# Near scores on full rows one head at a time, fewer opening dummies and a newly computed order in a one-core attention and convolution layer

## The chip, the cores and the metric

The kernel runs on 1 core of one Trainium2 chip. The metric is the device time of one execution in microseconds (us), as the median over the runs. Beside it stands one profiled execution with its trace; shares and durations come from that one.

## What is computed

One decoder layer over 1024 tokens of width 1024: a pre-norm, one combined input projection to 5632 columns, two branches, one output projection, the residual and a final norm. The attention branch mixes three dilated causal windows (128 with step 1, 512 with step 4, 2048 with step 16) by their softmax denominators; 16 query heads share 4 key heads. The convolution branch is a gated depthwise convolution of 31 taps, a layer norm and a gate.

```python
h = rmsnorm(x, norm_g)
proj = einsum('bsd,de->bse', h, w_in)            # 1024 x 1024 x 5632
q, k, v, a_gate, c_val, c_glu, c_gate = split(proj)
for window, dilation in ((128, 1), (512, 4), (2048, 16)):
    s = q k^T + alibi, causal and within the window, every dilation-th key
    m = max(s); p = exp(s - m); l = sum(p); o = p v / l; lse = m + log(l)
y_att = sum(softmax(lse) * o) * silu(a_gate)
c = conv1d(c_val * sigmoid(c_glu), conv_w) + conv_b
y_conv = silu(layernorm(c)) * silu(c_gate)
out = rmsnorm(x + concat(y_att, y_conv) @ w_out, final_norm_g)
```

## The kernel before

All float32 products are made of rounded parts. A value is split into a high part (fp32r) and a low part, the rest. A projection tile (`inproj`, tile names `ps`, `wh`, `wl`, `hhi`, `hlo`) adds three products of 512 columns into one PSUM bank, so that one block of 128 output columns takes 48 matmuls.

Attention works by pairs of heads (`attend(p)`, p from 0 to 7). The near scores of a query block of 128 tokens are taken against 256 keys, the far scores against every fourth key. The stationary operand of a score is `qs` (near) or `qf` (far): for head j of the pair, the 64 rows `r` from j x 64 hold the high part of the query, the other 64 rows its low part. `kdh` holds the high part of the keys on both halves of the rows, `kdl` their low part on both halves. In `score`, `first` is one matmul over all 128 rows for each unit (high and low query with the high key), and `second` adds the high query with the low key over 64 rows alone: rows 0 to 63 for head 0, rows 64 to 127 for head 1, so that `zip(*second)` issues the two heads' 64-row matmuls side by side. Each head has a PSUM bank of its own (`sc`, two in all). A near step has two query blocks of both heads: four full-row matmuls and then four of 64 rows, and it occurs four times for each pair, 32 times in all. The first of the four steps contains block 0, which has 128 keys in place of 256. On VectorE `add_min` then adds the bias and takes the least, and ScalarE takes the exponential.

Near and far results are exchanged through DRAM, the weights are transposed on TensorE (`tp_m`, `tp_s`, `tp_w`, `tp_p`), multiplied with the values (`on`, `of`) and gathered in `comb`.

The order of the whole program is written out by a planner, `Plan.order`. Every operation has an engine, a cost in us and a priority, its number less a boost (`pl.boost`, from `TUNE`). The planner takes the operation that can start first by its own model, and the program then holds each engine to that order. An engine's queue is in order, so whatever waits at its head holds up all behind it. The model counts for a DMA 1.1 us to its start, its bytes by a rate, and 0.9 us until its result counts as there (L395 to L397). `LIMITS` says how many buffers of a kind may be in use; most of them come from 33 slots of 4 KB a partition (`c4`). `SECTIONS` says which projection blocks (h and k, q, v, a, c by number) run beside which pair's attention: entry k runs beside `attend(k - 1)`, for k from 1 to 8; the convolution of `hc` k runs beside entries 0 to 7.

At the opening TensorE runs `WARM` transposes of the identity into a bank that nobody reads (tile `idle`), while the first rows of `x` come in. Behind them in its queue is the product that spreads `norm_g` over the partitions (`gbc`), for which the first scaling of `x` on VectorE waits. `MORE` adds dummies behind the transposes (`xT`) of the first two token blocks. `parameters` loads the convolution's rows (`rows`) with five small loads and transposes them (`par_ps`).

Near the end come `load_wo_att` (raw loads `raw_oa`, split into `woah` and `woal`), `layer_norm` by halves (`cc`, `mean`, `ss`, `var`, `rb`), the attention's output projection `att_part` (tile `opsa`, operand `ya` loaded from `y_dram`), and the convolution's (`opsc`). The load of `ya` names the last `woal` as something it comes after: `pl.load(y, ..., after=w[1][1][7] if last else z)`.

Of the kernel before, what the change touches and what calls it, by code (L numbers as in the profile page):

```python
# [31 lines left out]

LIMITS = {"x": 5, "raw": 1, "raw_oc": 1, "raw_oa": 2, "wh": 3, "wl": 3, "tab": 2, "e": 7, "pt": 4, "vs": 4, "vc":
          4, "turn": 2, "opsa": 2, "score": 2, "hc": 5, "c": 7, "t": 1, "g": 1, "gl": 7, "y": 2, "ag": 4, "cc": 5,
          "qs": 5, "qf": 4, "kdh": 9, "kdl": 6, "yc": 2, "ya": 2, "zc": 7, "za": 3}

RESERVE = {"e": 7, "pt": 3}
BANKS = {"mm": 3, "sc": 2, "tp": 2, "o": 1}  # L40
WARM = 55
LATE = C_CG + 6 * P
MORE = (10, 12)
TUNE = {"w": 195, "use": 240, "ln": 65, "att": 240, "conv": 5, "wo": 215, "woa": -20, "ap": 0, "wait": 0.2116}
SECTIONS = [("k0 q0 h1 v", 0), ("h2 a0 q1", 1), ("h3 a1 q2 a2", 1), ("q3 h4", 1), ("h5 k1 a3 q4", 1), ("h6 a4 q5",
            1), ("c0 h7 a5 q6", 1), ("c1 q7 a6 a7 c2 c3", 1), ("c4 c5", 1), ("c6 c7", 0)]


def score_tables():
# [112 lines left out]
class Plan:  # L162
    LATENCY = 0.2
    ahead = 267
    near = 574
# [138 lines left out]
    def order(self):  # L304
# [12 lines left out]
        held, inuse, taken, bank = set(), {}, {}, {}  # L317
# [7 lines left out]
        dma, table = 0.0, None  # L325
        out = []
        reserving = [i for i, op in enumerate(ops) if any(b.group in RESERVE for b in op[4])]
        first, last = reserving[0], reserving[-1]
# [31 lines left out]
        while len(out) < n:  # L360
            best = None
            for e, todo in ready.items():
                now, pick = None, None
                for i in sorted(todo, key=self.prio.__getitem__):
                    t = start_of(i)
# [12 lines left out]
            t, i = best  # L378
            e, cost, _, _, bufs = ops[i]
# [14 lines left out]
            done = end + self.LATENCY  # L394
            if e in ("SP", "POOL"):  # L395
                dma = max(dma, t + 1.1) + self.dma_time[i]
                done = dma + 0.9  # L397
            elif e == "DVE":
                done = end + 0.13
            for b in bufs:  # L400
# [63 lines left out]
def layer_kernel(tc, x, norm_g, w_in, conv_w, conv_b, ln_g, ln_b, w_out, fin_g, tab, out):  # L464
# [3 lines left out]
    def pool(name, space=None):  # L468
# [4 lines left out]
    pl = Plan(tc, {  # L473
        "big": (sb, "big", 4), "c8": (sb, "c8", 1), "c4": (sb, "c4", 33), "c2": (sb, "c2", 5), "st": (sb, "st", 16),
        "sx": (sb, "sx", 6),
        **{k: (ps, k, BANKS[k]) for k in PSUM_KINDS},
    }, LIMITS)

# [38 lines left out]
    def bank(kind, name, group=None):  # L517
        return pl.buf(kind, [P, 512], F32, name, group=group)
# [35 lines left out]
    raw, ready = {}, {}  # L554
# [106 lines left out]
    vs = [c4([P, 2, NKV, P], f"vs{i}", F32R) for i in range(4)]  # L661
    vc = [c4([P, 2, NKV, P], f"vc{i}", F32R) for i in range(4)]
# [39 lines left out]
    qs, qf = {}, {}  # L702
# [20 lines left out]
    ag = {}  # L723
# [15 lines left out]
    hc = {}  # L739
# [56 lines left out]
    def attend(p):  # L796
# [4 lines left out]
        kh, kl = kd[kv]  # L801
        y = c4([P, 4, 256], f"y{p}")
# [30 lines left out]
        def score(name, units):  # L833


            first, second, todo = [], [[], []], []
            for j in range(2):
                sc, o = bank("sc", f"sc{p}_{name}_{j}", "score"), 0
                for q, keys, t, e, s, near in units[j]:
                    dst = sc[:, o:o + e.cols]  # L840
                    to, r = dst.crossed() if near else dst, slice(j * DH, j * DH + DH)
                    first.append((to, q, keys(kh), not o, False))
                    second[j].append((to, q[r], keys(kl)[r], False, len(second[j]) == len(units[j]) - 1))
                    todo.append((e, dst, t, s))
                    o += e.cols
            pl.mm(first + [c for both in zip(*second) for c in both])
            for e, dst, t, s in todo:
                pl.add_min(e, dst, t, 3e38, s[:, 0])
                pl.act(e, e, AF.Exp, bias=s[:, 0], scale=-1.0, accum=s[:, 1])
# [13 lines left out]
        w = pl.buf("sx", [P, 4, 2, 2, 4], F32, f"w{p}")  # L863
        f = pl.buf("sx", [P, 4, 2, 4], F32, f"f{p}")
# [8 lines left out]
        both = f[:, :, 1, :]  # L873
# [291 lines left out]
```

## Time and profile before

| | us |
|---|---|
| median of 3 runs | 899.86 |
| lowest and highest | 898.11, 900.07 |
| profiled execution, device time | 898.14 |
| its span in the trace | 896.3 |
| TensorE busy in the span | 873.2 |
| VectorE busy | 655.8 |
| ScalarE busy | 592.8 |

The span is the time from the first to the last record of the core; 1.84 us of the profiled execution lie around it. A busy TensorE is not one at its peak, since matmuls are pipelined and their records overlap: the distance from one matmul's start to the next one's is what it costs the engine.

### The profile page before, as it was taken

The page shows a single profiled execution, that of the slowest core. Times are in us where ns is not written, and L with a number is a line of the kernel's source. Part 1 is how long each engine was busy: PE and PEld are TensorE (multiplying, and loading weights), DVE is VectorE, ACT ScalarE, POOL GpSimd, SP SyncE. Part 2 cuts the span into 40 slices and gives each one's busy share as a digit, 9 for nine tenths or more (in the row PEclk, how much of TensorE's full clock was granted, in tenths as well). Part 3 has the DMA queues.
Part 4 walks back from the last instruction along what each step waited for, and adds up shares of the span by engine and source line. Part 5 has one row for each costly group of instructions (what it writes and reads, how often), then busy time and mean ns, then how long its engine had stood idle before and what let it go on. Part 6 is the DMA issues. An engine that isn't in the chain of part 4 may idle for free.

```text
span 896.3 us, 13046 instructions
## 1 busy us (share of the span) xinstructions
PE 873.2 (97%) x4493; PEld 720.2 (80%) x4493; DVE 655.8 (73%) x1506; ACT 592.8 (66%) x1392; POOL 53.3 (6%) x69
## 2 busy tenths in 40 slices
PE   8999999999999999999999999999999799999996
PEld 7888888888888788887887887888787678878885
DVE  5769996689699689789989779943649895625333
ACT  4777368677958867977977947983896744414111
POOL 0001001010010010010010110101000000000000
PEclk9999999999999999999999999999999799999999
DMA  7533607254553474545355744455773697777111
GB/s 266 164 71 58 153 3 165 50 116 77 138 111 81 100 150 108 139 71 143 78 112 143 165 94 130 89 137 112 217 261 141 204 363 238 252 217 229 71 48 47
DMA packets 104953, 123.53 MB, mean 138 GB/s; under 512 B 17941, under 2 KB 78357, under 8 KB 104888
## 3 DMA queue, kind: packets, MB, share of 16 engines
q1 hardware_dynamic: 97000, 94.40, 34.3%
q0 software_dynamic: 7888, 28.32, 17.9%
q8 instruction: 35, 0.57, 0.3%
q14 instruction: 30, 0.25, 0.1%
HBM read 65.35 MB, written 24.84 MB: 101 GB/s over the span
## 4 chain that ended last, share of the span: by engine, by line
PE 86%; DMA 7%; DVE 3%; ACT 2%; issue 1%; SPq 1%; POOL 0%; DVEq 0%; ACTq 0%; POOLq 0%
PE ps L237 52%; PE opsc L237 10%; PE opsa L237 7%; PE sc_near L237 3%; PE on L237 3%; PE of L237 3%; PE sc_far L237 2%; DMA y<-comb 2%; PE tp_p L235 1%; PE tp_m L235 1%; DMA rows<-in_ln_b 1%; PE tp_s L235 1%; DMA raw_oc<-in_w_out 1%; ACT e L252 1%; DMA yc<-yc_dram 1%; DMA x<-in_x 1%
## 5 line engine op out<-in xcount | busy, mean ns | idle before, releaser
L237 PE MATMUL ps<-hhi,wh 128*128 128x512 f32 (+1 forms) x720 | 288.1, 401 | 0.3 <-ACT hhi L250 0.2
L237 PE MATMUL ps<-hlo,wh 128*128 128x512 f32 (+1 forms) x720 | 279.6, 390 | 0.3 <-DVE hlo L265 0.3
L237 PE MATMUL ps<-hhi,wl 128*128 128x512 f32 (+1 forms) x720 | 188.7, 395 | 0.0
L237 PEld LDWEIGHTS ps<-hhi,wh 128*128 128x128 f32 x720 | 135.6, 188 | 31.4 <-issue 0.5
L237 PEld LDWEIGHTS ps<-hlo,wh 128*128 128x128 f32 x720 | 135.8, 189 | 27.6 <-DVE hlo L265 0.8
L237 PEld LDWEIGHTS ps<-hhi,wl 128*128 128x128 f32 x720 | 129.3, 188 | 27.9
L252 ACT ACTIVATE e<-e,near 128x256 f32<-128x256 f32 (+1 forms) x256 | 115.6, 488 | 22.2 <-DVE near L265 12.3
L269 DVE SCALAR_TENSOR_TENSOR c<-hc,taps,c 128x511 f32<-128x511 f32 (+14 forms) x120 | 88.4, 737 | 0.3
L269 DVE SCALAR_TENSOR_TENSOR c<-t,taps,c 128x511 f32<-128x511 f32 (+14 forms) x120 | 88.6, 738 | 0.0
L269 DVE SCALAR_TENSOR_TENSOR t<-hc,taps,t 128x511 f32<-128x511 f32 (+6 forms) x112 | 82.5, 736 | 0.8 <-ACT t L252 0.8
L237 PE MATMUL opsc<-woc,yhc 128*128 128x512 f32 (+1 forms) x272 | 80.8, 381 | 0.0
L252 ACT ACTIVATE e<-e,far 128x224 f32<-128x224 f32 (+1 forms) x128 | 54.0, 424 | 36.0 <-DVE far L284 35.7
L298 POOL DMA_DIRECT2D wl<-raw x40 | 34.7, 868 | 452.1 <-ACT wl L252 350.1
L237 PEld LDWEIGHTS opsc<-woc,yhc 128*128 128x128 f32 x272 | 50.2, 188 | 10.6
L252 ACT ACTIVATE fjunk<-zc 128x512 bf16<-128x512 f32 (+1 forms) x17 | 10.3, 606 | 68.0 <-DVE zc L265 67.8
L237 PE MATMUL opsc<-woc,ylc 128*128 128x512 f32 (+1 forms) x136 | 52.0, 382 | 1.5 <-DVE ylc L265 1.5
L284 DVE CUSTOM_DVE_ANT_0 e<-sc_near,tab 128x256 f32<-128x256 f32 (+1 forms) x128 | 45.0, 404 | 9.9 <-PE sc_near L237 9.2
L250 ACT CAST wh<-raw 128x1024 fp32r<-128x1024 f32 x44 | 46.0, 1044 | 1.6 <-DMA raw<-in_w_in 1.4
L237 PE MATMUL opsa<-woah,yla 128*128 128x512 f32 x112 | 45.5, 406 | 1.5 <-DVE yla L265 1.5
L237 PE MATMUL opsa<-woah,yha 128*128 128x512 f32 x112 | 45.4, 405 | 0.0
L237 PE MATMUL opsa<-woal,yha 128*128 128x512 f32 x112 | 45.0, 402 | 0.0
L252 ACT ACTIVATE e<-e,f 128x96 f32<-128x96 f32 (+1 forms) x128 | 44.5, 439 | 0.2 <-DMA f<-back 0.2
(166 smaller groups left out, 1405.1 us busy)
## 6 DMA issues: line engine op xcount, KB each, us to landing
raw<-in_w_in SPq DMA_DIRECT2D x44, 512.0 KB, 4.5
wl<-raw POOLq DMA_DIRECT2D x40, 512.0 KB, 4.9
x<-in_x SPq DMA_DIRECT2D x8, 512.0 KB, 8.5
tab<-in_tab SPq DMA_DIRECT2D x8, 512.0 KB, 3.4
c_dram<-c SPq DMA_DIRECT2D x8, 512.0 KB, 3.3
g_dram<-g SPq DMA_DIRECT2D x8, 512.0 KB, 2.8
raw_oa<-in_w_out SPq DMA_DIRECT2D x8, 512.0 KB, 5.7
raw_oc<-in_w_out SPq DMA_DIRECT2D x8, 512.0 KB, 7.4
```

What stands on the lines that cost most here:

```text
L235: nc.tensor.transpose(out.ap(), a.ap(), b.ap())
L237: nc.tensor.matmul(out.ap(), a.ap(), b.ap(), start=start, stop=stop)
L250: nc.scalar.copy(out.ap(), x.ap())
L252: nc.scalar.activation(out.ap(), x.ap(), func, **{k: ap_of(v) for k, v in kw.items()})
L269: lambda: self.nc.vector.scalar_tensor_tensor(out.ap(), a.ap(), ap_of(s), b.ap(), op0, op1),
L284: lambda: self.nc.vector.tensor_tensor_reduce(out.ap(), a.ap(), b.ap(), 1.0, ap_of(first), ALU.add, ALU.min, least.ap()),
L298: self.op("POOL", 1.0, lambda: self.nc.gpsimd.dma_start(ap_of(dst), x.ap(), accum_op=ALU.add), [dst], [x, dst])
```

## The change

In `score`, a near unit is no longer put into `first` and `second`. For each head a list `one` takes, unit by unit, the full-row matmul with `kdh` and right behind it a full-row matmul with `kdl`, and each head's list is an operation of its own. (The low query times the low key comes along with it.) Far units stay as they were, over 64 rows side by side. `WARM` goes from 55 to 26 and `MORE` from (10, 12) to (8, 8). The planner counts 1.9 in place of 0.9 us at the end of a DMA. Limits, priorities and sections are other numbers: the loads and splits of `load_wo_att` have a boost of -350 in place of -20, `att_part` one of 50 in place of 0; the blocks a2 and c3 move by one section to later ones, `yc` has one buffer in place of two, `tab` one in place of two.

```diff
 LIMITS:
-  "wh": 3, "tab": 2, "hc": 5, "qs": 5, "kdl": 6, "yc": 2, "zc": 7
+  "wh": 4, "tab": 1, "hc": 7, "qs": 6, "kdl": 5, "yc": 1, "zc": 8
-WARM = 55
+WARM = 26
-MORE = (10, 12)
-TUNE = {"w": 195, "use": 240, "ln": 65, "att": 240, "conv": 5, "wo": 215, "woa": -20, "ap": 0, "wait": 0.2116}
-SECTIONS = [("k0 q0 h1 v", 0), ("h2 a0 q1", 1), ("h3 a1 q2 a2", 1), ("q3 h4", 1), ("h5 k1 a3 q4", 1), ("h6 a4 q5",
-            1), ("c0 h7 a5 q6", 1), ("c1 q7 a6 a7 c2 c3", 1), ("c4 c5", 1), ("c6 c7", 0)]
+MORE = (8, 8)
+TUNE = {"w": 225, "use": 120, "ln": 75, "att": 240, "conv": 15, "wo": 165, "woa": -350, "ap": 50, "wait": 0.2116}
+SECTIONS = [("k0 q0 h1 v", 0), ("h2 a0 q1", 1), ("h3 a1 q2", 1), ("a2 q3 h4", 1), ("h5 k1 a3 q4", 1), ("h6 a4 q5",
+            1), ("c0 h7 a5 q6", 1), ("a6 c1 a7 q7 c2", 1), ("c5 c4 c3", 1), ("c6 c7", 0)]
...
                 dma = max(dma, t + 1.1) + self.dma_time[i]
-                done = dma + 0.9
+                done = dma + 1.9
...
             for j in range(2):
-                sc, o = bank("sc", f"sc{p}_{name}_{j}", "score"), 0
+                sc, o, one = bank("sc", f"sc{p}_{name}_{j}", "score"), 0, []
                 for q, keys, t, e, s, near in units[j]:
                     dst = sc[:, o:o + e.cols]
                     to, r = dst.crossed() if near else dst, slice(j * DH, j * DH + DH)
                     first.append((to, q, keys(kh), not o, False))
-                    second[j].append((to, q[r], keys(kl)[r], False, len(second[j]) == len(units[j]) - 1))
+                    last = len(todo) % len(units[j]) == len(units[j]) - 1
+                    if near:
+                        one += [first.pop(), (to, q, keys(kl), False, last)]
+                    else:
+                        second[j].append((to, q[r], keys(kl)[r], False, last))
                     todo.append((e, dst, t, s))
                     o += e.cols
-            pl.mm(first + [c for both in zip(*second) for c in both])
+                if one:
+                    pl.mm(one)
+            if first:
+                pl.mm(first + [c for both in zip(*second) for c in both])
```

## Rows read from the trace of the kernel before

**Rows 1.** The page: busy time of the engines, and TensorE's granted clock in 40 slices.

```profile
PE 873.2 (97%) x4493; PEld 720.2 (80%) x4493; DVE 655.8 (73%) x1506; ACT 592.8 (66%) x1392; POOL 53.3 (6%) x69
PEclk9999999999999999999999999999999799999999
```

**Rows 2.** Busy time by stretch (start:end, length, each engine's, clock, DMA share, GB/s).

```profile
0.00:26.00 26.00, 21.71 (x146) 19.24 (x147) 14.82 (x31) 13.59 (x26) 1.02 (x8) 0.94 0.78 259
270.00:330.00 60.00, 57.91 (x321) 47.66 (x320) 50.17 (x134) 52.13 (x137) 5.09 (x6) 1.00 0.44 103
693.00:709.00 16.00, 9.56 (x33) 7.01 (x32) 13.81 (x26) 12.42 (x18) 0.00 (x0) 0.68 0.77 243
```

**Rows 3.** Timeline of TensorE, a near step of full blocks (start, length, engine, line, operation).

```profile
132.66 0.63 PE L237 MATMUL sc_near<-kdh,qs 128*128 128x256 f32 x4
133.22 0.50 PE L237 MATMUL sc_near<-kdl,qs 64*128 64x256 f32 x4
133.65 0.50 PE L237 MATMUL ps<-hhi,wh 128*128 128x512 f32 x1
```

**Rows 4.** Timeline of TensorE, a near step that contains block 0.

```profile
269.20 0.62 PE L237 MATMUL sc_near<-kdh,qs 128*128 128x128 f32 x4
...
270.18 0.50 PE L237 MATMUL ps<-hhi,wh 128*128 128x512 f32 x1
```

**Rows 5.** Timeline at the opening, first and last of 13 full-row matmuls of 256 columns.

```profile
17.20 0.28 PE L237 MATMUL ps<-hlo,wh 128*128 128x256 f32 x1
...
18.61 0.28 PE L237 MATMUL ps<-hlo,wh 128*128 128x256 f32 x1
```

**Rows 6.** Timeline of TensorE, the short far scores: eight of full rows, then of 64.

```profile
71.51 0.99 PE L237 MATMUL sc_far<-kdh,qf 128*128 128x96 f32 x8
72.42 0.65 PE L237 MATMUL sc_far<-kdl,qf 64*128 64x96 f32 x8
```

**Rows 7.** Timeline of the opening (in brackets the idle time before, and who ended it).

```profile
1.45 8.23 PE L235 MATMUL idle<-ident 128*128 128x128 f32 x55 [1.45 <-POOL ident masks.py:199]
...
9.61 1.98 PE L237 MATMUL gbc<-gain,avg 1*128 1x512 f32 x4
...
10.77 2.92 DVE L269 SCALAR_TENSOR_TENSOR x<-x,xst,gbc 128x512 f32<-128x512 f32 x4 [2.42 <-PE gbc L237]
...
19.23 2.72 DVE L269 SCALAR_TENSOR_TENSOR x<-x,xst,gbc 128x512 f32<-128x512 f32 x4
...
21.54 0.66 PE L235 MATMUL par_ps<-ident,rows 34*128 34x34 f32 x8 [1.70 <-DMA rows<-in_ln_b]
...
22.12 1.50 PE L235 MATMUL xT<-ident,x 128*128 128x128 f32 x8
```

**Rows 8.** Busy time by stretch at the opening, columns as in rows 2.

```profile
1.40:5.60 4.20, 4.15 (x20) 4.15 (x21) 0.23 (x1) 1.94 (x4) 0.20 (x1) 1.00 0.81 276
...
22.60:26.10 3.50, 2.94 (x15) 2.54 (x14) 2.67 (x5) 2.80 (x8) 0.00 (x0) 0.51 0.75 219
```

**Rows 9.** Timeline of TensorE in the tail of the third pair's attention.

```profile
311.04 0.33 PE L235 MATMUL tp_w<-ident,e 128*128 128x128 f32 x1 [1.19 <-ACT e L252]
```

**Rows 10.** Timeline around the layer norm's first half: DMA issues on SP, and TensorE.

```profile
682.11 0.33 SPq L301 DMA_DIRECT2D g_dram<-g  x1
...
683.02 0.73 SPq L295 DMA_DIRECT2D cc<-c_dram  x1
...
696.07 0.39 SPq L295 DMA_DIRECT2D ya<-y_dram  x1
...
700.48 2.05 PE L237 MATMUL rb<-ident,lst 128*128 128x128 f32 x8 [4.28 <-DVE lst L269]
```

**Rows 11.** Busy time by stretch, columns as in rows 2: TensorE's half clock there.

```profile
698.50:708.80 10.30, 7.39 (x21) 5.78 (x22) 8.73 (x18) 9.00 (x13) 0.00 (x0) 0.50 0.90 279
```

**Rows 12.** DMA issues: tile, queue, count, KB each, median us from issue to landing.

```profile
raw_oa<-in_w_out SPq DMA_DIRECT2D x8, 512.0 KB, 5.7
raw_oc<-in_w_out SPq DMA_DIRECT2D x8, 512.0 KB, 7.4
```

More of the change, by code (lines that the diff above doesn't have):

```diff
@@ L29 @@
 C_Q, C_K, C_V, C_AG, C_VAL, C_GLU, C_CG = 0, 1024, 1280, 1536, 2560, 3584, 4608
-LIMITS = {"x": 5, "raw": 1, "raw_oc": 1, "raw_oa": 2, "wh": 3, "wl": 3, "tab": 2, "e": 7, "pt": 4, "vs": 4, "vc":
-          4, "turn": 2, "opsa": 2, "score": 2, "hc": 5, "c": 7, "t": 1, "g": 1, "gl": 7, "y": 2, "ag": 4, "cc": 5,
-          "qs": 5, "qf": 4, "kdh": 9, "kdl": 6, "yc": 2, "ya": 2, "zc": 7, "za": 3}
+LIMITS = {"x": 5, "raw": 1, "raw_oc": 1, "raw_oa": 2, "wh": 4, "wl": 3, "tab": 1, "e": 7, "pt": 4, "vs": 4, "vc":
+          4, "turn": 2, "opsa": 2, "score": 2, "hc": 7, "c": 7, "t": 1, "g": 1, "gl": 7, "y": 2, "ag": 4, "cc": 5,
+          "qs": 6, "qf": 4, "kdh": 9, "kdl": 5, "yc": 1, "ya": 2, "zc": 8, "za": 3}
 RESERVE = {"e": 7, "pt": 3}
 BANKS = {"mm": 3, "sc": 2, "tp": 2, "o": 1}
-WARM = 55
+WARM = 26
 LATE = C_CG + 6 * P
-MORE = (10, 12)
-TUNE = {"w": 195, "use": 240, "ln": 65, "att": 240, "conv": 5, "wo": 215, "woa": -20, "ap": 0, "wait": 0.2116}
-SECTIONS = [("k0 q0 h1 v", 0), ("h2 a0 q1", 1), ("h3 a1 q2 a2", 1), ("q3 h4", 1), ("h5 k1 a3 q4", 1), ("h6 a4 q5",
-            1), ("c0 h7 a5 q6", 1), ("c1 q7 a6 a7 c2 c3", 1), ("c4 c5", 1), ("c6 c7", 0)]
+MORE = (8, 8)
+TUNE = {"w": 225, "use": 120, "ln": 75, "att": 240, "conv": 15, "wo": 165, "woa": -350, "ap": 50, "wait": 0.2116}
+SECTIONS = [("k0 q0 h1 v", 0), ("h2 a0 q1", 1), ("h3 a1 q2", 1), ("a2 q3 h4", 1), ("h5 k1 a3 q4", 1), ("h6 a4 q5",
+            1), ("c0 h7 a5 q6", 1), ("a6 c1 a7 q7 c2", 1), ("c5 c4 c3", 1), ("c6 c7", 0)]
 def score_tables():
```

## The prediction

> **What bounds the kernel now.** I read the page first: TensorE is busy for 97% of the span, VectorE for 73%, ScalarE for 66%, and TensorE's clock is granted in full but for one dip in slice 31 [rows 1]. So TensorE sets the time, and an edit counts in two ways only: by what it takes out of TensorE's own stream, or by a stretch in which TensorE has nothing to do. The second view is the busy time by stretch. The reader should compare the length of a stretch with TensorE's busy time in it: three stretches fall short, the opening by 26.0 - 21.7 = 4.3 us, the tail of the third pair's attention by 60.0 - 57.9 = 2.1 us, and the layer norm's first half by 16.0 - 9.6 = 6.4 us [rows 2]. In the last one the clock is at 1.2 GHz, half its level elsewhere, for 10.3 us, with 7.4 us of busy time, so that some 3.7 us of work time are lost beside the idle 6.4 [rows 11]. The third view is the timeline, for the pitch of matmuls and for who waits at these places.
>
> The sums are made against the profiled execution, 898.14 us, of which 1.84 lie outside its span. The median of the runs, 899.86, is 1.72 above it; I add that at the end.
>
> **Near scores, a certain small gain.** A step of full blocks takes 133.65 - 132.66 = 0.99 us from its first matmul to the next work: 0.56 for the four full-row ones, 0.43 for the four of 64 rows [rows 3]. Full-row matmuls of 256 columns follow each other by (18.61 - 17.20)/12 = 0.1175 us [rows 5]. Eight of them make 0.94 us, 0.05 less. Of 32 steps 24 are of this kind: 1.2 us. A step with block 0 takes 0.98 us [rows 4]. Afterwards it has four matmuls of 128 and four of 256 columns. The nearest row for short full-row ones is the far score of 96 columns, eight in 72.42 - 71.51 = 0.91 us, 0.114 each, hardly less than 256 columns take [rows 6]. At that pitch the step takes 0.91 us, a gain of 0.07; if the columns alone counted (0.0588 and 0.1175) it would take 0.71, a gain of 0.27. I take 0.07, since the far row shows short ones held up, and 8 steps give 0.6. Sum: 1.8 us, bounds 1.2 and 3.4. All of it lies on the path, because TensorE is the bound.
>
> Here a rule of the Trainium skill speaks against the change. The rows show that the side-by-side pass of four 64-row matmuls costs 0.43 us where four full-row ones cost 4 x 0.1175 = 0.47, so pairing buys almost nothing once the way in and out is counted [rows 3, 5]. The page "TensorEngine Tiling (Array Packing)", section "Theoretical Speedup", gives a factor of up to 2 for a contraction of 64 or less; by that the old pass would take 0.24 us, and the change would cost 0.23 us a step, some 7 us in all. The same page's "Key Properties" says that a change of tiling mode drains the engine. The trace agrees with the second and not with the first.
>
> That each head is an operation of its own lets VectorE begin on head 0 after four matmuls rather than after all eight. VectorE and ScalarE are not the bound, so I count it at nothing; their slack of a quarter to a third of the span hides it [rows 1]. Were they the bound at such a place, it would help, not hurt.
>
> **Opening.** 55 dummies occupy TensorE from 1.45 to 9.6 us. The first 20 of them take 4.15 us, the other 35 the remaining 4.0: half rate until 5.6 and full rate from there [rows 7, 8]. With 26 the last ends near 5.6 + 6 x 0.117 = 6.3. `gbc` follows at once, 1.16 us from its start to VectorE's (10.77 - 9.61), so its first bank is there at 7.5. VectorE's first scaling waited 2.42 us for it, so it could have begun at 8.35 [rows 7]. That makes the start 2.4 us earlier. What is next late: the third block's transposes began at 22.12, though their first operand was done at about 19.23 + 0.7 = 19.9. In front of them in TensorE's queue stood `par_ps`, which waited for the last small load [rows 7]. If the new order leaves that so, the 2.4 us are waited away there: 0. If it moves `par_ps` back, 2.4 + 2.2 = 4.6 are to be had. Counting a DMA 1 us longer makes the planner put users of loads later, so I take the middle, 2.3. The clock fell to half at 22.6 for 3.5 us here, with 2.94 us busy [rows 8]; if that goes, or comes at a dearer place, it is 1.5 us either way. The six dummies fewer of `MORE` are 6 x 0.117 = 0.7 us between transposes that wait for VectorE anyway: nothing, at most 0.7. Bounds: a loss of 1.5, a gain of 6.
>
> **Blocks moved between sections.** A projection block is 48 matmuls of 512 columns, 48 x 2 x 0.1175 = 11.3 us of work for TensorE. a2 moves from beside the second pair to beside the third, whose tail is where TensorE idles 2.1 us while it waits on ScalarE's scaled weights [rows 2, 9]. The cover is larger than the hole, and the second pair's stretch had none; I take 1.5, bounds 0 and 2.1. c3 moves to beside the last pair, so everything ahead of it can come up to 11.3 us sooner in TensorE's queue while the last projection ends at the same place.
>
> **Layer norm's first half.** TensorE's own work ran out at 693 us, and it stood until `rb` at 700.48, which waited 4.28 us for the statistics [rows 10]. These were late because the last load of `cc` was issued at 683.02, on SP behind a store of `g_dram` at 682.11 that waited for a gate. The first `ya`, without which the output projection can't begin, went out at 696.07, since it comes after the last `woal`. The planner held these loads to be quicker than they are: 1.1 + 1.75 + 0.9 = 3.75 us for 512 KB by its own constants, where the trace has 5.7 and 7.4 us to landing [rows 12]. With 1.9 it counts 4.75, still too low but nearer. c3 held back, `woa` at -350 (slots and SP go to the layer norm first) and `ap` at 50 all act here. All that can be won is 6.4 + 3.7 = 10.1 us. I take 4, less than half, because the same -350 delays what `ya` waits for. Bounds: a gain of 10, a loss of 10 (second rival).
>
> **The rest of the order** is anew too, and no row shows it. Outside the three stretches TensorE idles hardly at all, so there is little to win and something to lose; I charge 1.6 us for new small waits, about three quarters of the one hole that the old order left in the attention part [rows 2], bounds 0 and 5. `yc` with one buffer: its load and split lie beside a token block's 48 matmuls, again 11.3 us, and cost nothing as long as load and split together stay below that; the table's nearest loads land in 5.7 to 7.4 us [rows 12].
>
> **Sum.** 898.14 - 1.8 - 2.3 - 1.5 - 4.0 + 1.6 = 890.1 for a profiled execution, and 891.9 with the 1.72: I say 892, 0.9% faster.
>
> **Rivals.**
> First, the layer norm's hole closes altogether, because the gates held back and the earlier statistics keep TensorE at work through it: 6 us more than counted, 886. For it speaks that the moved block (11.3 us) is longer than the hole; against it that the projections' end and the last `woal` are both still needed before `opsa`.
> Second, slower: the attention's output weights come late. With -350 the raw loads and splits of `w_out` give way to everything else on SP, ScalarE and VectorE; all `ya` loads wait on the last split, so TensorE ends its projections and stands, partly at half clock afterwards as now. In the old order the first `ya` went out some 3 us after TensorE's projections ended. Each further us costs one, or 1.5 with the clock. The edits before it give 1.8 + 2.3 + 1.5 - 1.6 = 4.0, so the kernel gets slower by more than 0.2% once this hole grows by 6 us, that is, when the first `ya` is issued over 8 us behind the last projection. At 10 us more: 899.9 - 4.0 + 10 = 906. For it speaks that VectorE is busy for 13.8 of the 16 us there [rows 2]; against it that the planner counts these operations and their engines, and only the DMAs wrongly.
> Third, nothing to measure: the opening's gain is waited away behind `par_ps`, the new order trades one small hole for another, and only the near scores' 1.8 us remain: 898.
> Last, that the added full-row passes cost more than rows 5 let expect: at 0.17 us each in place of 0.1175, 0.21 us a step over 32 steps, 6.7 us, which leaves 899, no change. The first half of each near step has the same shape and shows 0.56 us for four, with the way into the 64-row pass in it [rows 3], so I give it little.
>
> **Chances.** Forecast 0.48 (887 to 895), hole closed 0.18, nothing to measure 0.13 with the dearer full rows (0.03) in it, slower 0.21. Of the forecast's and first rival's 0.66 all is faster by over 0.2% (1.8 us, about what a measurement of this kernel can tell from no change). That gives 0.66, 0.13 and 0.21. The range goes from 884, the first rival with the opening's upper bound in part, to 904, short of the slower rival's middle: about 0.1 is left out on either side.
>
> **What would show it.** In the changed kernel's trace: near steps without 64-row matmuls and with eight at a pitch near 0.117 us (wrong if it is 0.14 or more); VectorE's first scaling at about 8.4 us with no wait on `gbc`; the third block's transposes before 20 us (right) or behind `par_ps` at 21 or later (waited away); TensorE full from 270 to 330; and from the last projection to the first `opsa` a gap well below 9 us, with the clock's dip gone or shorter. The prediction is wrong if that gap has grown, if a dip to half clock appears in a stretch of dense projections, or if TensorE idles over 2 us at places where it didn't.

## The result and the profile after

| | before | after |
|---|---|---|
| median of 4 runs, us | 899.38 | 883.04 |
| lowest, highest | 898.11, 900.07 | 882.07, 884.46 |
| profiled execution | 898.14 | 883.03 |
| its span | 896.3 | 881.3 |

The ratio is 0.9821, 95% interval 0.9803 to 0.9839: 1.8% faster, 9 us under the forecast of 892 and 1 us under the low end of the range. The span is 15.0 us shorter.

The page of the kernel after, the lines that answer to [rows 1]:

```profile
PE 865.1 (98%) x4458; PEld 722.5 (82%) x4458; DVE 654.7 (74%) x1506; ACT 591.7 (67%) x1392; POOL 53.3 (6%) x69
PEclk8899999999999999999999999999999999999999
```

The dip in slice 31 is gone; two shallower ones stand at the opening. Busy time by stretch, columns as in [rows 2]:

```profile
0.00:26.00 26.00, 20.80 (x113) 17.95 (x113) 15.06 (x30) 13.57 (x24) 1.03 (x8) 0.79 0.80 261
270.00:330.00 60.00, 59.91 (x326) 50.42 (x325) 49.75 (x109) 47.79 (x116) 5.96 (x7) 1.00 0.52 115
463.00:475.00 12.00, 10.18 (x54) 8.35 (x53) 11.70 (x44) 11.10 (x41) 0.91 (x1) 0.86 0.70 159
690.00:709.00 19.00, 18.56 (x83) 14.48 (x82) 13.65 (x25) 12.34 (x18) 0.00 (x0) 1.00 0.58 187
```

The third pair's tail (second line) and the layer norm's first half (fourth) are now full. A stretch that was full falls short, 463 to 475 us. TensorE's longest waits (what waited, for whom: us in total, times, longest):

```profile
PE par_ps L235 <- DMA rows<-in_ln_b: 3.1, 1, 3.1
PE sc_near L237 <- DVE near L284: 1.6, 2, 1.0
PE idle L235 <- POOL ident masks.py:199: 1.5, 1, 1.5
PE opsc L237 <- ACT yhc L250: 0.8, 1, 0.8
```

To place the 15 us I added up, in either trace, the columns of the matmuls in the order of their starts, each at its full-row pitch and without the dummies, and read off when the same sum had been issued. The difference after minus before grows like this:

| part of the work | us |
|---|---|
| opening, to about 58 us | +0.9 |
| first pairs, to 300 us | -1.7 |
| third pair's tail, 300 to 324 us of before | -3.1 |
| to 461 us | -0.7 |
| 461 to 486 us of after | +2.9 |
| to 692 us of before | -2.7 |
| layer norm's first half, 692 to 724 us of before | -9.7 |
| to the end | -1.0 |

### The profile page after: what moved, and what is told of

Its sections match the earlier page's. It is cut to its first block, busy times and chain, and to the rows that moved or that the text cites. A ratio compares the mean times of both kernels' runs of the same rounds, so it can differ in the third digit from the quotient of the medians.

```text
span 881.3 us, 12967 instructions
## 1 busy us (share of the span) xinstructions
PE 865.1 (98%) x4458; PEld 722.5 (82%) x4458; DVE 654.7 (74%) x1506; ACT 591.7 (67%) x1392; POOL 53.3 (6%) x69
## 4 chain that ended last, share of the span: by engine, by line
PE 88%; DMA 4%; DVE 3%; issue 2%; ACT 1%; SPq 0%; POOL 0%; ACTq 0%; POOLq 0%
PE ps L237 51%; PE opsc L237 10%; PE opsa L237 8%; PE sc_near L237 3%; PE on L237 3%; PE sc_far L237 3%; PE of L237 3%; PE tp_p L235 2%; PE tp_m L235 1%; DMA rows<-in_ln_b 1%; PE tp_s L235 1%; DMA yc<-yc_dram 1%; DMA x<-in_x 1%; PE tp_w L235 1%; DMA wl<-raw 1%
## 5 line engine op out<-in xcount | busy, mean ns | idle before, releaser
L237 PEld LDWEIGHTS ps<-hhi,wh 128*128 128x128 f32 x720 | 137.6, 191 | 27.0
L237 PEld LDWEIGHTS ps<-hlo,wh 128*128 128x128 f32 x720 | 137.6, 191 | 26.3 <-DVE hlo L265 0.7
L252 ACT ACTIVATE e<-e,f 128x224 f32<-128x224 f32 (+1 forms) x128 | 45.2, 438 | 0.0
```

The lines of the kernel that those rows point to most:

```text
L237: nc.tensor.matmul(out.ap(), a.ap(), b.ap(), start=start, stop=stop)
L252: nc.scalar.activation(out.ap(), x.ap(), func, **{k: ap_of(v) for k, v in kw.items()})
```

## Experiments

Between the groups of runs the kernel before stood at 898.8 to 902.6 us (single executions from 896.7 to 906.5), so kernels are compared by their ratios to it, or by spans. Its profiled execution, 898.14 us, is one of the shorter ones: a ratio can therefore show up to 5 us more gain than the difference of spans, and two changed kernels are better compared by their spans and medians. "At equal work" is the reading just described.

### What leaving a 64-row pass costs

`e1_near`: the kernel before with its own order; only the emission of a near step changes, to full rows head by head.

```diff
-            pl.mm(first + [c for both in zip(*second) for c in both])
+            pl.mm(old, emit)    # planned as before, issued as:
+            emit += [first[k], (first[k][0], q, keys(kl), False, u == len(units[j]) - 1)]
```

> The kernel before with its own order, instruction for instruction; only the near steps are issued as the changed kernel issues them: for each head, unit by unit, the full-row matmul with kdh and then a full-row one with kdl. My theory (the prediction's first term): a full step takes 0.94 us in place of 0.99, one with block 0 0.91 in place of 0.98, in all 1.8 us less (1.2 to 3.4), 0.2%, ratio 0.998. Rival (the added passes cost what their columns cost and the pairs cost half): 0.2 us more a step, some 7 us more, ratio 1.007. Second rival: the near scores carry a large part of the 16 us that the change brought (a head's bank free sooner lets VectorE and ScalarE run ahead): 5 us or more less, ratio below 0.995.

Measured: 892.74, ratio 0.9905 [0.9868, 0.9941], span 891.4, 4.9 less. At equal work the gain comes as 0.6 us a pair, from the first pair to the last, and the layer norm's hole stays. A step takes 0.94 us in place of 0.99, as forecast, which explains 0.05. The rest stands one row further than [rows 3]. (`e1_near` itself has the same times: a step from 133.03 to 133.97, and 0.24 us from the matmul behind it to the next.) First the row of the kernel before that follows there, then a step of the kernel after:

```profile
133.99 0.40 PE L237 MATMUL ps<-hlo,wh 128*128 128x512 f32 x1
```
```profile
126.98 0.28 PE L237 MATMUL sc_near<-kdh,qs 128*128 128x256 f32 x1
...
127.80 0.28 PE L237 MATMUL sc_near<-kdl,qs 128*128 128x256 f32 x1
127.92 0.40 PE L237 MATMUL ps<-hhi,wh 128*128 128x512 f32 x1
128.16 0.39 PE L237 MATMUL ps<-hlo,wh 128*128 128x512 f32 x1
```

Behind the 64-row pass the next matmul holds TensorE for 133.99 - 133.65 = 0.34 us, behind a full-row one for 128.16 - 127.92 = 0.24. A step thus gains 0.05 + 0.10 to 0.11, and 32 steps 5 us. The number is the one that the second rival named; its mechanism, a head's bank free sooner, isn't needed for it, since the two prices in the steps themselves add up to the whole gain. The first rival, 7 us more, is out.

`e11_far` asks the same of the 16 far steps of 224 columns, in the order of `e8_a2` (below).

```diff
-                pl.mm(first + [c for both in zip(*second) for c in both])
+                pl.mm(first + [...], emit)    # issued head by head on full rows if units[0] has two units
```

> As e8_a2, with its order; the far steps of 224 columns (16 in all) are issued like the near ones, each head's full-row matmuls with kdh and kdl in turn, while the short ones of 96 columns stay side by side. Theory (the way into and out of the 64-row pass costs, the matmul behind it included): such a step takes 0.94 us to the next matmul's start and that one 0.11 us more than its like; with eight full-row ones at 0.11 it takes 0.89, so 0.15 us less a step, 2.4 us in all, 876.4, ratio 0.97 to 0.974. Rival (as in the prediction's own count, only the step itself): 0.05 us a step, 0.8 us in all, 878. Third (the pairs are worth their halved columns): 2 us more.

Measured: 876.08, ratio 0.9734 [0.9707, 0.9760], span 874.9 against 877.2: 2.3 less, as the corrected sum said. A far step of the kernel after, then one of this kernel:

```profile
463.49 0.60 PE L237 MATMUL sc_far<-kdh,qf 128*128 128x224 f32 x4
...
464.42 0.50 PE L237 MATMUL ps<-hhi,wh 128*128 128x512 f32 x1
464.76 0.40 PE L237 MATMUL ps<-hlo,wh 128*128 128x512 f32 x1
```
```profile
121.84 0.27 PE L237 MATMUL sc_far<-kdh,qf 128*128 128x224 f32 x1
...
122.72 0.41 PE L237 MATMUL ps<-hhi,wh 128*128 128x512 f32 x1
122.97 0.39 PE L237 MATMUL ps<-hlo,wh 128*128 128x512 f32 x1
```

0.93 + 0.34 becomes 0.88 + 0.25: 0.14 a step, 16 x 0.14 = 2.2.

### The layer norm's hole

`e5_c3` is the kernel after with c3 back beside the seventh pair, `e9_c3_before` the kernel before with c3 beside the last pair, `e6_woa` the kernel after with -20 for `load_wo_att`.

```diff
-("a6 c1 a7 q7 c2", 1), ("c5 c4 c3", 1)          # e5_c3
+("a6 c1 a7 q7 c2 c3", 1), ("c5 c4", 1)
-("c1 q7 a6 a7 c2 c3", 1), ("c4 c5", 1)          # e9_c3_before
+("c1 q7 a6 a7 c2", 1), ("c4 c5 c3", 1)
-"woa": -350                                     # e6_woa
+"woa": -20
```

> The changed kernel with c3 back beside the seventh pair, as before; order computed anew. Theory (moved blocks close the layer norm's hole): TensorE runs out of projections before the attention's output projection can start, a hole of 5 us or more with a half-clock stretch comes back there, and the time is 890 to 894 (ratio 0.990 to 0.994). Rival (the order of the last stage, not the block, closed it): within 1.5 us of the changed kernel, ratio 0.981 to 0.983.

> The kernel before with c3 alone moved from beside the seventh pair to beside the last; scores, dummies, priorities, limits and the planner's DMA time as before, order computed anew. Theory (the moved projections alone keep TensorE at work through the layer norm's first half): the idle 6.4 us and the 10 us at half clock at 693 us go, 8 to 15 us less than before, ratio 0.984 to 0.991. Rival (it needs the new priorities and the longer DMA time as well): the hole stays, because the output weights and the statistics come as late as they did: ratio 0.996 to 1.002.

> The changed kernel with the boost of the attention's output weights at -20 in place of -350. Theory (the weights' low priority gives buffers and queues to the layer norm and is part of what closed the hole): the last load of cc and the statistics come later, a hole of 4 us or more before rb or the first opsa returns, 888 or more, ratio 0.988 or above. The prediction's slower rival, the other way round: earlier weights start opsa sooner, 882 or less. Null: within 1.5 us.

Measured: `e5_c3` 897.5 (expected at most 894), ratio 0.9966 [0.9944, 0.9988], span 896.8; `e9_c3_before` 892.26, 0.9908 [0.9873, 0.9943], span 892.0; `e6_woa` 883.0, 0.9811 [0.9773, 0.9849], span 880.7. At equal work `e5_c3` loses 15.6 us, 15 of them at the layer norm; `e9_c3_before` gains 6.5 there and gives 2 back at other places. The boost does nothing that the runs can tell. Issues on SP and TensorE's matmuls around the hole, first the kernel after, then `e5_c3`, then `e9_c3_before`:

```profile
684.65 0.97 SPq L295 DMA_DIRECT2D ya<-y_dram  x2
...
688.52 0.95 PE L237 MATMUL var<-avg,ss 128*128 128x1 f32 x8
...
689.88 0.80 PE L237 MATMUL opsa<-woah,yha 128*128 128x512 f32 x1
...
701.50 1.05 PE L237 MATMUL rb<-ident,lst 128*128 128x128 f32 x8
```
```profile
689.20 0.95 PE L237 MATMUL var<-avg,ss 128*128 128x1 f32 x8
...
691.16 0.39 SPq L295 DMA_DIRECT2D ya<-y_dram  x1
...
696.09 2.04 PE L237 MATMUL rb<-ident,lst 128*128 128x128 f32 x8 [4.97 <-DVE lst L269]
```
```profile
693.81 0.98 SPq L295 DMA_DIRECT2D ya<-y_dram  x2
...
695.59 0.95 PE L237 MATMUL var<-avg,ss 128*128 128x1 f32 x8
...
699.64 1.13 PE L237 MATMUL rb<-ident,lst 128*128 128x128 f32 x8 [2.15 <-DVE lst L269]
```

In all three `var` follows the last projection. In the latter two `rb` starts 6.9 and 4.1 us behind `var`, and TensorE has only 1.1 us of other work between them (`mean`). In the kernel after the first `ya` is issued 3.9 us ahead of `var`, so `opsa` can run from 689.88, and `rb` is put behind 11.6 us of it. In `e5_c3`, as in [rows 10], `ya` goes out behind the projections, nothing is ready, TensorE stands 5 us, and its clock is at 1.2 GHz afterwards (0.51 from 694.9 to 705.3 us). So the hole closes only with c3's place. The place isn't enough by itself: `e9_c3_before` keeps a wait of 2.15 us, and `e16_pairs` (below), which has c3 moved too, loses 6.2 us here. That its 11.3 us of projection now lie behind what `ya` needs, instead of ahead of it, fits these rows; `e9_c3_before` has `ya` in time as well (1.8 us ahead of `var`), but `rb` still ahead of `opsa`.

### Parts that only work together

The planner's numbers (`LIMITS`, `TUNE`, the order inside two sections), the 1.9 us of a DMA, and c3. `e12_near_c3` is the kernel before with the near scores of after and c3 moved. `e13_plus_dma` adds the 1.9 to it, `e15_numbers` the numbers of after, `e14_dummies` both. All four have a2 and the dummies where they were before. `e10_dma_before` is the kernel before with 1.9 alone, `e7_dma` the kernel after with 0.9.

```diff
-                done = dma + 0.9      # e10_dma_before, e13_plus_dma; the other way in e7_dma, e15_numbers
+                done = dma + 1.9
```

> The kernel before with two parts of the change: the near scores as the changed kernel has them, and c3 beside the last pair. Dummies, priorities, limits, a2 and the planner's DMA time as before; order computed anew. Theory (these two carry the change: 5 us for the near scores, the hole at the layer norm for c3): the hole in the last stage is closed or nearly so, 884 to 890, ratio 0.982 to 0.989, most of the change's 0.982. Rival (the priorities and the longer DMA time are needed to keep the last stage free of new waits): the near scores' 5 us and c3's 7 to 8 as measured alone don't add, the last stage has other waits, 891 or more, ratio above 0.990.

> The kernel before with the changed kernel's near scores, c3 moved to beside the last pair, and 1.9 us counted at the end of a DMA; limits, priorities, dummies and all else are those of before. The two without the 1.9 gave 894.2. Theory: the longer DMA time is what takes the scattered waits away once c3 is moved; then the time is 882 to 886, and the waits of opsa for cc and yla, 4 us together, are gone. Rival: on its own it only shifts them, as it did on the kernel before (+3 us); then 892 to 898, with a wait of TensorE for yla or cc of over 2 us left behind the layer norm.

> As the kernel just described (near scores, c3 moved, dummies of before, the changed limits and priorities) but with 0.9 us counted at the end of a DMA. Theory that the longer DMA time is what is needed: waits for yla and cc behind the layer norm, 884 to 888, as the 0.9 cost 5 us in the changed kernel. Rival, that the limits and priorities do it: within 2 us of the kernel with 1.9, 878 to 881.

> The kernel before with only the planner's DMA time at 1.9 in place of 0.9 us. The prediction's reasoning (a truer DMA time puts users of loads later and takes waits out of in-order queues): 2 to 6 us less, most of it at the opening and after 690 us, ratio 0.993 to 0.998. Rival (with the blocks where they were, the last stage is short of work for TensorE whatever the planner believes of loads): within 0.2% of before, the hole at 693 us in place.

> The changed kernel with the planner counting 0.9 us at a DMA's end, as before. Theory (a planner that holds loads to be quicker than they are puts their users at the head of in-order queues): waits on loads in the last stage and at the opening come back, 886 to 892, ratio 0.985 to 0.992. Rival: the numbers of sections and priorities decide, 881.5 to 884.5, ratio 0.980 to 0.984.

Measured, ratio to the kernel before (median in us):

| near scores and c3 of after, with | 0.9 us for a DMA | 1.9 us |
|---|---|---|
| the numbers of before | 0.9919 [0.9890, 0.9949] (894.17) | 0.9983 [0.9964, 1.0003] (901.18) |
| the numbers of after | 0.9889 [0.9866, 0.9913] (893.29) | 0.9713 [0.9688, 0.9737] (877.30) |

`e10_dma_before` gave 902.26, 1.0030 [1.0012, 1.0048], where 2 to 6 us less were expected; `e7_dma` 887.86, 0.9864 [0.9822, 0.9905]. So the 1.9 costs 0.6% with the old numbers and gains 1.8% with the new; the numbers gain 0.3% without it, which the intervals don't tell from nothing, and 2.7% with it. My theory for `e13_plus_dma` (882 to 886) was wrong, its rival (892 to 898) still too low, and the theory of `e15_numbers` right in sign and too small in size. Near scores (span -4.9) and c3 (-4.3) alone do not add up to `e12_near_c3` either (-3.9). The waits show where. TensorE's in `e13_plus_dma`, `e15_numbers` and `e14_dummies`:

```profile
PE opsa L237 <- DVE yla L265: 9.7, 2, 8.2
PE rb L237 <- DVE lst L269: 3.4, 2, 2.1
PE var L237 <- DVE ss L265: 2.8, 1, 2.8
```
```profile
PE opsa L237 <- DVE yla L265: 4.5, 3, 2.7
...
PE sc_near L237 <- DVE near L284: 1.4, 1, 1.4
PE par_ps L235 <- DMA rows<-in_ln_b: 1.3, 1, 1.3
```
```profile
PE idle L235 <- POOL ident masks.py:199: 1.5, 1, 1.5
PE opsc L237 <- DVE ylc L265: 1.1, 1, 1.1
PE xT L235 <- issue: 0.7, 1, 0.7
```

With one of the two the output projection still waits for the split of `ya` (`yla`), once for 8.2 us with 17 us at half clock around it (733.5 to 750.5 us); with both no wait above 1.5 us is left anywhere. Why the planner's choices come out so, operation by operation, was not followed.

### The opening

`e2_warm`: the order of before, 26 dummies in front. `e3_rows`: the kernel after with the five small loads issued right behind that of `gain`. `e4_rows_dummies`: that, with the dummies behind the transposes where `MORE` puts them (in the kernel after the planner put all 42 in front). `e14_dummies`, already in the table, is `e8_a2` with the dummies of before.

```diff
-    pl.mm([(idle[:, 0:P], ident, ident, None, None)] * WARM)
+    pl.mm(dummy * WARM, dummy * 26)                         # e2_warm: planned as 55, 26 issued
+        return seq[:k] + self.early + seq[k:]               # e3_rows: small loads behind gain's
+            seq.insert(seq.index(behind) + 1, i)            # e4_rows_dummies: dummies behind xT
-WARM = 26                                                   # e14_dummies
+WARM = 55
-MORE = (8, 8)
+MORE = (10, 12)
```

> The kernel before with its own order; only the first block of dummies has 26 transposes in place of 55, the ten and twelve behind stay where they were. Theory: VectorE's first scaling starts at about 8.4 us in place of 10.8, the first projection matmul some 2 us sooner, but par_ps still waits for the last small load until 21 us or later and the rest waits behind it: time within 0.7 us of before, ratio 0.999 to 1.001. Rival (the prediction's term): 2.3 us less, ratio 0.9974. Second rival: TensorE has less to do before 16 us, the clock falls to 1.2 GHz in the opening as in the changed kernel, and the time is 1 us longer or more, ratio 1.001 or above.

> The changed kernel with its own order; only the five small loads of the convolution's parameters are issued on SP right behind the load of norm_g, ahead of the third block of x. Theory: in the changed kernel TensorE stands 3.1 us before par_ps, waiting for the last of these loads, which SP issued at 10.7 us and then for 6 us; with them early that wait is gone, the second half of the opening comes 2 to 3 us sooner, and 880 to 881 us result, ratio to before 0.979. Rival: the opening is bound by the loads of x and of the first weights, and the wait turns up at the next operand: 882.5 to 883.5, ratio 0.982.

> As e3_rows, and of the 42 dummies that the changed kernel's order has in one block at the front, 8 stand behind the transposes of the first block of x and 8 behind those of the second, as the program text writes them (26 in front). Theory: gbc starts at about 6.3 us in place of 7.8 and the stretch at half clock from 11.7 to 18.5 us goes, so that the first block's projections run at 0.12 us a matmul in place of 0.24: a further 1 to 2 us, 879, ratio 0.9775. Rival: that work waits for VectorE and for x in any case, and the time is that of e3_rows within 0.5 us; or the clock falls all the same.

> The changed kernel with a2 put back beside the second pair (878.8) and the opening's dummies of before, 55 in front and 10 and 12 behind the transposes. Theory: the opening is bound by its loads, so the later start costs nothing; 878 to 880. Rival: the start 3.5 us earlier is worth its time here, since this order lets the casts begin sooner; then 881 to 883.

Measured: `e2_warm` 899.6, ratio 0.9984 [0.9958, 1.0009], span 898.0 (+1.6); the interval holds no change and the 2.3 us less alike, so it is the trace that decides here. `e3_rows` 884.01, 0.9800 [0.9771, 0.9830], span 882.2 (+0.9 on the kernel after); `e4_rows_dummies` 883.68, 0.9800 [0.9770, 0.9830], span 881.8: neither brought what its theory had, 2 to 4 us, and the clock was at 1.2 GHz for 6.8 us of the opening in the one and 10.2 in the other. `e14_dummies` 877.30 with span 875.3, against 877.2 for `e8_a2`. The kernel after in its opening:

```profile
7.82 1.98 PE L237 MATMUL gbc<-gain,avg 1*128 1x512 f32 x4
...
8.18 1.04 ACT L250 CAST wh<-raw 128x1024 fp32r<-128x1024 f32 x1 [0.48 <-DMA raw<-in_w_in]
...
8.98 2.92 DVE L269 SCALAR_TENSOR_TENSOR x<-x,xst,gbc 128x512 f32<-128x512 f32 x4 [0.49 <-PE gbc L237]
...
18.69 1.03 PE L235 MATMUL xT<-ident,x 128*128 128x128 f32 x8
...
22.88 1.04 PE L235 MATMUL par_ps<-ident,rows 34*128 34x34 f32 x8 [3.15 <-DMA rows<-in_ln_b]
```

The scaling starts 1.8 us sooner than in [rows 7] and the third block's transposes 3.4 us, but `par_ps` now waits at 22.88, and by 10 us of work the kernel is 1.0 behind. Without that wait, in `e3_rows`, the weights are what is late:

```profile
14.25 1.04 ACT L250 CAST wh<-raw 128x1024 fp32r<-128x1024 f32 x1 [7.00 <-DMA raw<-in_w_in]
...
18.17 0.58 PE L237 MATMUL ps<-hhi,wh 128*128 128x256 f32 x1 [4.71 <-ACT hhi L250]
```

In these kernels an earlier start is thus given back to whichever loads are late. `e14_dummies` starts `gbc` at 11.06, 1.9 us behind `e8_a2`, and is 1.9 us ahead of it from 27 us on: neither of its two expectations, which were no change and a loss. Busy time by stretch, first in `e8_a2`, then in `e14_dummies`:

```profile
21.10:28.10 7.00, 5.08 (x28) 5.05 (x29) 4.83 (x8) 4.32 (x9) 0.00 (x0) 0.51 0.81 230
```
```profile
21.10:28.10 7.00, 6.43 (x51) 5.58 (x52) 5.96 (x10) 5.66 (x10) 0.00 (x0) 1.00 0.83 225
```

`e8_a2` waits 3.0 us for `par_ps` and has 7 us at 1.2 GHz; `e14_dummies` has neither. What each is worth is told by the start of `par_ps`, first in `e8_a2`, then in `e14_dummies`:

```profile
23.02 1.03 PE L235 MATMUL par_ps<-ident,rows 34*128 34x34 f32 x8 [2.96 <-DMA raw<-in_w_in]
```
```profile
22.65 0.65 PE L235 MATMUL par_ps<-ident,rows 34*128 34x34 f32 x8
```

With 1.9 us of head start `e8_a2` comes out of its wait 0.4 us later. The other 1.5 us arise behind this point, where its matmuls of 256 columns follow each other by 0.21 us in place of 0.12. `e2_warm` shows the same against the kernel before: `gbc` 3.5 us sooner, `par_ps` at 21.88 after a wait of 4.5 us, against 21.54 [rows 7], and behind it 1.2 GHz for 6.8 us, against 3.4, and 1.5 us more lost. So the wait uses up the head start, and the clock behind the wait makes the loss.

### The place of a2

`e8_a2` is the kernel after with a2 back beside the second pair. `e18_a2_dummies` is `e14_dummies` with a2 moved, as in the kernel after.

```diff
-("h3 a1 q2", 1), ("a2 q3 h4", 1)
+("h3 a1 q2 a2", 1), ("q3 h4", 1)
```

> The changed kernel with a2 back beside the second pair. Theory: the idle 2 us in the tail of the third pair's attention return, 2 to 3 us more, 885 to 886, ratio 0.984 to 0.986, and the stretch between the fifth and sixth pair, where the changed kernel lost 3 us, is as in the changed kernel. Rival: the tail is covered by other blocks: within 1 us of the changed kernel.

> The changed kernel with the dummies of before (55 in front, 10 and 12 behind the transposes), a2 beside the third pair as in the changed kernel; against the 877.3 of the kernel that differs in a2's place alone. Theory: moving a2 costs some 4 us in this order too, because the fifth and sixth pairs' near scores again meet with no projection between them; 881 to 883 with a hole near 465 us. Rival: the hole was an accident of one order, and a2's place is worth no more than 1 us either way; 876 to 878.

Measured: `e8_a2` 878.79, ratio 0.9763 [0.9726, 0.9800], span 877.2; `e18_a2_dummies` 882.37, 0.9815 [0.9759, 0.9870], span 879.1 against 875.3. Both ways a2 beside the third pair costs 4 us: the theory of `e8_a2` (2 to 3 us more) was wrong and so was its rival (no change), while that of `e18_a2_dummies` came true. What it saves, the tail of the third pair, is 0.5 to 0.9 in these orders. What it costs stands at 463 to 475 us. TensorE in the kernel after:

```profile
466.36 0.28 PE L237 MATMUL sc_near<-kdl,qs 128*128 128x256 f32 x1
467.22 0.36 PE L237 MATMUL sc_near<-kdh,qs 128*128 128x256 f32 x1 [0.58 <-DVE near L284]
...
468.91 0.41 PE L237 MATMUL sc_near<-kdh,qs 128*128 128x256 f32 x1 [0.97 <-DVE near L284]
469.12 0.41 PE L237 MATMUL sc_near<-kdl,qs 128*128 128x256 f32 x1
```

The sixth pair's near steps follow each other with no projection between them, so each waits for VectorE to empty its bank, and the clock is at half from 469.06 to 472.5 us. With a2 back, the same 12 us are full (busy 12.00). Why a block moved at the second pair shows at the sixth was not followed.

### Near scores inside the changed kernel, and the best kernel

`e16_pairs` is the kernel after with `score` of before, its order computed anew.

```diff
-                    if near:
-                        one += [first.pop(), (to, q, keys(kl), False, last)]
-                    else:
-                        second[j].append((to, q[r], keys(kl)[r], False, last))
+                    second[j].append((to, q[r], keys(kl)[r], False, len(second[j]) == len(units[j]) - 1))
```

> The changed kernel with the near scores as before: four full-row matmuls, then four of 64 rows side by side, both heads in one operation; the order computed anew with that. Theory: 32 steps at 0.16 us, 5 us dearer than the changed kernel, 888, spread as some 0.6 us a pair; the layer norm's stage unchanged. Rival: what the near scores win in TensorE's stream is small beside what the order makes of it; then the difference is not 5 (under 2 or over 8) and sits at single stalls of over 1 us.

Measured: 888.53, ratio 0.9839 [0.9817, 0.9862], span 886.0, 4.7 longer than the kernel after. The total is the theory's, the places are the rival's, so that the total agrees by luck. At equal work only 1.5 us come from 118 to 441 us, where five pairs at 0.64 would give 3.2 (in the kernel after, three near steps there take 1.05 to 1.11 us instead of 0.94); the hole at 463 us is absent, which gains 3.8; and 6.2 us are lost at the layer norm, where `rb` again stands ahead of `opsa`:

```profile
692.03 1.13 PE L237 MATMUL rb<-ident,lst 128*128 128x128 f32 x8 [3.06 <-DVE lst L269]
```

`e17_best` is `e14_dummies` with the far steps of `e11_far`.

> The kernel with a2 beside the second pair and the dummies of before (877.3), and in it the 16 far steps of 224 columns issued head by head on full rows, in the same order of operations. Since no order changes, theory: the same 2.3 us as where this was tried before, 875.0, ratio 0.969. Rival: the opening's other order has left waits of which the shorter far steps only bring on the next; under 1 us, 876.5 or more.

Measured: 875.57, ratio 0.9735 [0.9689, 0.9781], span 873.0 against 875.3: 2.3 less, as in `e11_far`. (The ratio is no better than the 0.9713 of `e14_dummies` because the kernel before stood at 898.84 us in this group and at 902.62 in that one; the medians are 875.57 and 877.30. It leads `e11_far`, 876.08, by 0.5 us in the medians and 1.9 in the spans.) This edit leaves the order alone, and its price carried over from one order to another.

## Why the prediction was right and wrong

The sum had 8.0 us, the span fell by 15.0. Term by term, the near scores by `e1_near` and taken out of the other rows of the reading at equal work (rounded, so the sum is off by 0.1):

| term | forecast, us | measured, us |
|---|---|---|
| near scores | -1.8 | -4.9 |
| opening | -2.3 | +0.9 |
| third pair's tail | -1.5 | -3.1 |
| layer norm's first half | -4.0 | -9.7 |
| the rest of the order | +1.6 | +1.7 |

The result left the range because of the layer norm's term above all: 5.7 of the 7 us. The gain of the near scores was put 3.1 too low and that of the opening 3.2 too high, and that these two cancel is luck.

**The bound** was read rightly: what helped took time out of TensorE's stream or filled a stretch in which it stood.

**Near scores**: right in sign, 1.8 forecast, about 5 measured (`e1_near`), above the upper bound of 3.4. The term was mis-sized because the sum ended at the start of the matmul behind the pass. That matmul's 0.50 us in [rows 3], against 0.40 for its like, was the sign that its own cost had grown by 0.11. The way out was named in the prediction, and priced only up to that matmul's start. The page "TensorEngine Tiling (Array Packing)" of the Trainium skill, section "Key Properties", says that a change of tiling mode drains the engine. This trace shows a price at both changes, 0.56 - 4 x 0.1175 = 0.09 us on the way in and 0.10 to 0.11 on the way out; that a drain makes it is not shown. The rival of dearer full rows fell: the pitch is 0.1175 us (126.98 to 127.92 in 8).

**Opening**: 2.3 to be gained, 0.9 lost. I had two cases, a gain waited away behind `par_ps` and one kept if `par_ps` moved back. It moved back and waited there. The step that failed was to move one waiter and count its wait as won, when what it waits for is a queue of loads; the DMA share of the stretch is 0.78 before and 0.80 after. At equal work the kernel is 2.8 us ahead at the third block's transposes and still 0.3 ahead once past `par_ps`; from there the clock, at 1.2 GHz for 6.8 us in place of 3.4, makes a loss of it. The 1.5 us that the prediction gave to the clock were right in size. VectorE's first scaling came at 8.98 us, not 8.4, because all 42 dummies stand in front. And one of the named signs of being wrong came: 1.2 GHz from 11.7 to 18.5 us, with TensorE busy for 6.41 of 6.80 us in the first projections.

**a2**: the third pair's tail did close, by 3.1 us. But 1.9 of them are there in `e8_a2` too, with a2 beside the second pair, so a2 isn't what closed most of it. A gain was booked for filling the tail, and the price of taking a block out of the second pair's stretch was set at nothing. It is 4 us, elsewhere (`e8_a2`, `e18_a2_dummies`).

**Layer norm**, the step that failed most: 4 forecast, 9.7 measured: the first rival, at 0.18, came true. The largest winnable sum, 10.1, was right. I halved it because -350 would hold up `ya`; `e6_woa` shows that this boost does nothing (span 880.7 against 881.3), and `ya` came 11 us sooner. I also looked for the cure in earlier statistics. It was in `opsa` being ready to run ahead of `rb`. The second rival's own measure, the first `ya` against the last projection, was the right one to watch; it came out on the other side of it.

**The rest of the order**: +1.6 forecast for new small waits, +1.7 measured, and that is luck: one hole of 3.5 us came (2.9 in the table above, which has 0.6 of near scores in it), the price of a2's place, and the other places gave about 1.8 back. That the 1.9 by itself is no gain (`e10_dma_before`) and yet carries the order (`e7_dma`, `e15_numbers`) was in no step of mine: I costed the parts of the order one by one, and the runs show that they can't be.

The one buffer for `yc` cost nothing that shows: TensorE's waits for `yhc` and `ylc`, the parts of `yc`, come to 1.3 us, against 1.5 before.

## What to carry to other kernels

Cost a step up to the start of the second matmul behind it: what a mode leaves behind is paid there. An idle engine behind the last projection is filled by whatever work is loaded by then, so ask first when that work's loads are issued, and only then how to shorten the chain it waits for. Numbers of a planner are costed together, by a run, and not as a sum of parts; the edits that left the order alone kept their price here (the far steps 2.3 us in two orders).

## What was not expected of the hardware

A 64-row pass of 256 or 224 columns, side by side, is dearer than full rows that compute twice as much: 0.43 + 0.11 us against 4 x 0.1175 = 0.47 in a near step. And an opening with 77 dummies, all at 2.4 GHz from 6.3 us on, overtook one with 42 that began its work 1.9 us sooner and was granted 1.2 GHz from 21.2 to 28.0 us.
